# Second layer: the third head's q and k projections listed ahead of the attention's first scores, around the transposes of the RWKV output

## The chip, the cores and the metric

One core of a Trainium2 chip runs the whole kernel; seven cores stand idle. The metric is the device time in microseconds (us) of one execution. The kernel before took 1156.28 us as the median of three runs, which were 1147.5, 1156.28 and 1362.1 us.

## What is computed

Two layers of a hybrid backbone run over 512 latent tokens and 256 context tokens of width 1024. Each layer normalises, modulates and projects the tokens once, then feeds three mixers: an RWKV-7 scan in both directions, a short convolution, and differential attention with four heads. Cut to what this case touches:

```python
h = rms_norm(x, pre_g) * (1.0 + scale[:, None, :]) + shift[:, None, :]
p_l = split_projection(h @ w_in)                  # latent; p_c the same for the context
y_rwkv_l, _ = rwkv_mixer(p_l[0:8], p_c[0:8], ...)  # scan, readout, times silu(z)
# differential attention, head by head: two score maps per head
s = einsum('bqhjd,bkhjd->bhjqk', q, k) * scale     # q and k with axial rotary positions
p = softmax(s, axis=-1)
attn = p[:, :, 0] - lam * p[:, :, 1]
o = einsum('bhqk,bkhe->bqhe', attn, v)             # then rms_norm, times silu(z)
y_l = concatenate([y_rwkv_l, y_conv_l, y_attn_l], axis=-1) @ w_out
```

In the second layer only the latent tokens are wanted at the end, so queries are 512 rows; keys are 512 latent and 256 context rows.

## The kernel before

All products run on TensorE in fp32r pairs: an operand is split into a high part and a low remainder, and one product takes three matmuls (high by high, low by high, high by low). `split` (L242 to L262) loads a weight piece of 128x512 on the queue of SyncE (L251, `wraw`), casts its high part on ScalarE (L258, `whi`) and subtracts on GpSimd (L261, `wlo`). Two `wraw` buffers and three `whi`/`wlo` pairs serve all pieces. One projection of 128 output channels (`proj_ch`) needs two pieces: 24 matmuls of 512 latent columns (`pcl`) and, for keys, 24 more of 256 context columns (`pcc`).

Projections are generators that are put on a list, `fq`. `fill(us)` draws so many nominal microseconds of matmuls from the front of that list, wherever the code wants TensorE to have something to do while another engine works. The scheduler then orders the instructions of each engine by program order as priority and by what its own model holds ready; inside the attention the matmuls are pinned to program order (`lin["on"]`).

For each head, `qk` (L1084 to L1102) projects q and then k, evicts them (ScalarE, L1090, `qkr`), copies rotated halves by four DMAs (L1095, `qks`), multiplies by the sine table on GpSimd (L1096) and by the cosine table on VectorE, adds, casts the high part on ScalarE (L1099), subtracts the low part on VectorE, and writes both parts to DRAM (L1101 and L1102, `qd`). `head_in` (L1135 to L1158) loads a head's parts back from there as `QS`, `KH`, `KL`.

The end of a layer goes so: `rwkv_scan`, then `rwkv_out`, which normalises the scan's output `Y` on VectorE, then calls `fill(F["o"])`, and transposes `Y` on TensorE (`yT`, 32 matmuls). Then come the first head's loads, `fill(1e9)` (everything that is left on the list), and `attention`. That one works on units of 128 query rows, x counting from -3: scores of unit x+3 into three PSUM banks (`sc`), row maxima on VectorE (`mx`), exponentials on ScalarE (`e`), the combination of both maps on VectorE and GpSimd, transposes (`aTp`) and the product with v (`av`). Up to x = -1, `scores` has only one buffer of three banks (`pr0`), so each unit's scores wait for the exponentials of the unit before. The second such buffer (`pr1`) takes the banks of the projections, once `fill(1e9)` at x = 0 has emptied the list. After `attention` stand the splits of the RWKV and convolution outputs (`y_split`: casts and subtractions into `lat` on VectorE and GpSimd), which the scheduler draws forward.

`attn_proj` returns three lists: q, k, v of heads one and two; the attention's gate (`z_gate`, four projections); and `[qk(2), qk(3)]`, the third and fourth head's q and k. Before the change the last list goes on `fq` just before `attention`. There, `fill(FA[0])` draws 16 us of it ahead of the first scores, and `fill(FA[1])` draws 6 us behind the scores of each of the first three units.

Of the kernel before, what the change touches and what calls it, by code (L numbers as in the profile page):

```python
# [51 lines left out]
ATB = 2  # L52
ORD = [(0,), (4, 5), (1,), (2,), (3,)]
F = dict(p=1.0, s=0.5, i=0.45, i2=0.45, m0=4, m3=3, m1=3, m2=4, a=0.2, b=0.6, c=0.4, n=0.6, o=8, o2=2)
FL = [dict(F), dict(F, p=1.2, c=0.19, n=0.38, m0=3.5, a=0.32, o=11.9)]
H0 = 99
KS = 3
MP = 'fc'
# [6 lines left out]
FA = (16,6)  # L65
# [41 lines left out]
def build(tc, A):  # L107
# [217 lines left out]
    def filler():  # L325
        while modq:
            try:
                next(modq[0])
                return
            except StopIteration:  # L330
                modq.pop(0)
# [63 lines left out]
    def chs(l, idxs):  # L395
        wseq.extend((l, 2 * i + j) for i in idxs for j in range(2))

    def toks(l, idx):
        wseq.extend((l, 2 * idx + j) for j in range(4))
# [56 lines left out]
    fq = []  # L456

    def fill(us):
        while us > 0 and fq:
            try:  # L460
                us -= next(fq[0])
            except StopIteration:
                fq.pop(0)
# [696 lines left out]
    def attention(l, lat, cx, pool, az_done, hd0):  # L1160
        last = l == L - 1
        li = 0.8 - 0.6 * math.exp(-0.3 * l)
        n = NL if last else NT
# [156 lines left out]
                heads[u["h"] + 1] = head_in(l, u["h"] + 1, pool)  # L1320

        lin["on"] = AL
        fill(FA[0])
        fins = []

        def at(i):
            return us[i] if 0 <= i < len(us) else None

        for x in range(-3, len(us)):
            u, p, c, e, w = at(x), at(x - 1), at(x + 1), at(x + 2), at(x + 3)  # L1330
# [122 lines left out]
    for l in range(L):  # L1453
        F.update(FL[l])
        last = l == L - 1
        n = NL if last else NT
# [20 lines left out]
        with tc.tile_pool(name=f"yy{l}", bufs=1, reuse_waits="tile") as yy:  # L1477
            with tc.tile_pool(name=f"rw{l}", bufs=1, reuse_waits="tile") as rw:
                if RO:
                    for tag, nw, nb in (("rT", 2 * NT, 1), ("pt", 512, PTB), ("km", 512, 3), ("bk", 1024, 2), ("iv", 512, 2),  # L1480
                                        ("Wv", 512, 1), ("od", 256, 2), ("invt", 112, 1), ("ms", 256, 1), ("zu", 256, ZUB), ("gs", 128, 2),
                                        ("pz", 128, 2), ("rt", 512, 2)):
                        rw.tile([P, nw], F32, tag=tag, bufs=nb, name="rsv")
                modq[:] = [mod_half(a, t, hf, rp[0], "R", pt="c") for a, t in ME[l] for hf in range(2)]
                st = rwkv_in(l, lat, cx, rw, yy, pre)
                while modq and not must:
                    filler()
                toks(l, I_V)
                chs(l, (I_ZR, I_ZR + 1))
                chs(l, range(I_CONV, I_CONV + 8))  # L1490
                ap1, ap2, az = attn_proj(l, lat, cx)
                fq[:] = must + [rwkv_v(l, lat, cx), z_gate(l, 2, zrd[l], 0.5, lat, cx), conv(l, lat, cx)] + ap1
                rwkv_scan(l, st, rw, lat, cx)
                fill(FO)
                modq[:] = [mod_half(a, t, hf, rw, "pt", pt="c") for a, t in ML[l] for hf in range(2)]
                fq.extend(ap2)
                yr = yy.tile([P, 2, NT], F32, tag="yr", name="yr")
                rwkv_out(l, st, yr, rw)
                if EH == 2:
                    hd0 = head_in(l, 0)  # L1500
                fill(1e9)
                if EH == 3:
                    hd0 = head_in(l, 0)
                while modq:
                    filler()
# [199 lines left out]
```

## Time and profile before

| | |
|---|---|
| median of three runs | 1156.28 us (1147.5 to 1362.1) |
| time of the profiled execution | 1150.33 us |
| its span, first to last instruction | 1148.3 us |
| TensorE busy | 1034.9 us, 90% |
| VectorE busy | 731.3 us, 64% |
| ScalarE busy | 523.7 us, 46% |
| GpSimd busy | 488.0 us, 42% |
| granted TensorE clock, mean | 0.973 |

Times in rows count from the span's start. The profiled execution's time is 2.0 us above its span. A row of the timeline names start, duration, engine, line, operation, output and inputs; brackets give the idle time before it and what ended it. A row that stands for several instructions gives their count. Line L134 is the helper through which matmuls are recorded, L118 that of VectorE, so tiles tell more than lines there.

### The profile page before, as it was taken

How to read it: one execution, taken by the hardware profiler on the slowest of the kernel's cores; microseconds unless marked ns; L12 is line 12 of the kernel's file. 1: busy time of each engine (PE TensorE's matmuls, PEld its weight loads, DVE VectorE, ACT ScalarE, POOL GpSimd, SP SyncE). 2: the span in 40 equal slices, each digit the busy share in tenths (PEclk: the TensorE clock that was granted, in tenths of full speed). 3: DMA queues.
4: the chain of work that ended last, by engine and by line, in shares of the span. 5: the costliest groups of instructions: out<-in, count | busy, mean ns of one | idle time of the engine just before them, and what ended most of it. 6: DMA issues, size and time to landing. Idle time of an engine off the chain costs nothing.

```text
span 1148.3 us, 25449 instructions
## 1 busy us (share of the span) xinstructions
PE 1034.9 (90%) x9850; PEld 847.2 (74%) x9850; DVE 731.3 (64%) x1712; ACT 523.7 (46%) x1330; POOL 488.0 (42%) x508
## 2 busy tenths in 40 slices
PE   4899989999798999989899899998987999888897
PEld 1577968777687877878787786866766897777775
DVE  3530658687666253499847857676986824579944
ACT  4332462452362232378723564654343533338731
POOL 1311534434625422464522346254474454456632
PEclk9899999999899999999999999999998999999999
DMA  9573322212423365754052452232232345555143
GB/s 350 182 245 121 89 73 57 61 31 87 141 73 112 121 189 175 223 165 108 15 188 74 147 167 88 71 100 78 72 97 85 92 132 150 165 158 170 47 156 110
DMA packets 92088, 142.55 MB, mean 124 GB/s; under 512 B 28192, under 2 KB 36416, under 8 KB 91968
## 3 DMA queue, kind: packets, MB, share of 16 engines
q1 hardware_dynamic: 88512, 136.14, 38.4%
q10 hardware_dynamic: 3456, 4.80, 1.3%
q8 instruction: 77, 1.26, 0.5%
q14 instruction: 43, 0.35, 0.1%
HBM read 110.99 MB, written 25.71 MB: 119 GB/s over the span
## 4 chain that ended last, share of the span: by engine, by line
PE 36%; DVE 24%; ACT 6%; issue 6%; POOL 4%; DMA 3%; SPq 1%; DVEq 0%; ACTq 0%; POOLq 0%
PE pcl L134 10%; PE op L134 6%; PE ptl L134 4%; DVE mx L118 4%; PE pcc L134 2%; PE ptc L134 2%; PE ch L132 2%; DVE e L118 2%; DVE bk L118 2%; DVE rs_t L118 1%; DMA mraw<-in_mod_w_dram 1%; DVE qkr L118 1%; POOL wlo L261 1%; PE av L134 1%; PE yps L132 1%
## 5 line engine op out<-in xcount | busy, mean ns | idle before, releaser
L261 POOL TENSOR_TENSOR wlo<-wraw,whi 128x512 fp32r<-128x512 f32 x134 | 181.9, 1360 | 312.2 <-ACT whi L258 279.4
L134 PE MATMUL pcl<-lat,whi 128*128 128x512 f32 (+1 forms) x928 | 295.3, 395 | 1.0 <-POOL lat L344 0.8
L134 PEld LDWEIGHTS pcl<-lat,whi 128*128 128x128 f32 x928 | 170.2, 190 | 40.2 <-issue 6.4
L134 PE MATMUL pcl<-lat,wlo 128*128 128x512 f32 (+1 forms) x464 | 185.1, 399 | 5.1 <-POOL wlo L261 3.7
L258 ACT CAST whi<-wraw 128x512 fp32r<-128x512 f32 x144 | 88.4, 618 | 159.8 <-DMA wraw<-in_w_in_dram 38.5
L134 PE MATMUL pcc<-ctx,whi 128*128 128x256 f32 x576 | 112.8, 292 | 2.0 <-DVE ctx L118 1.7
L134 PEld LDWEIGHTS pcl<-lat,wlo 128*128 128x128 f32 x464 | 88.0, 190 | 28.2 <-POOL wlo L261 5.6
L134 PEld LDWEIGHTS pcc<-ctx,whi 128*128 128x128 f32 x576 | 95.2, 197 | 9.0 <-issue 3.2
L134 PE MATMUL pcc<-ctx,wlo 128*128 128x256 f32 x288 | 84.4, 293 | 2.0 <-DVE wlo L118 2.0
L134 PE MATMUL ptl<-whi,lat 128*128 128x256 f32 x384 | 82.0, 299 | 1.1 <-ACT qkr L1090 1.1
L1222 ACT ACTIVATE e<-sc,mx 128x768 f32<-128x768 f32 (+1 forms) x80 | 66.5, 834 | 19.5 <-DVE mx L118 14.0
L118 DVE TENSOR_REDUCE mx<-sc 128x1 f32<-128x768 f32 (+1 forms) x72 | 63.7, 918 | 14.0 <-PE sc L134 14.0
L134 PE MATMUL av<-vA,aT 128*128 128x128 f32 x416 | 59.6, 287 | 14.0 <-ACT aT L1257 13.8
L134 PEld LDWEIGHTS av<-vA,aT 128*128 128x128 f32 x416 | 54.2, 195 | 20.9 <-ACT aT L1257 17.9
L134 PEld LDWEIGHTS ptl<-whi,lat 128*128 128x128 f32 x384 | 65.4, 201 | 3.4 <-ACT qkr L1090 1.4
L118 DVE TENSOR_TENSOR R<-s,cs 128x384 f32<-128x384 f32 (+1 forms) x96 | 47.0, 529 | 20.9 <-PE s L132 20.2
L134 PEld LDWEIGHTS pcc<-ctx,wlo 128*128 128x128 f32 x288 | 56.7, 197 | 4.6 <-DVE wlo L118 2.2
L134 PE MATMUL ptl<-wlo,lat 128*128 128x256 f32 x192 | 57.6, 300 | 0.0
L920 POOL TENSOR_TENSOR pz<-zu,pc 64x128 f32<-64x128 f32 x88 | 37.4, 425 | 45.9 <-DVE zu L118 41.1
L134 PE MATMUL sc<-KH,QS 128*128 128x256 f32 (+1 forms) x144 | 51.4, 371 | 4.7 <-ACT e L1222 2.9
L134 PE MATMUL sc<-KL,QS 128*128 128x256 f32 (+1 forms) x144 | 45.0, 334 | 0.0
L1233 POOL TENSOR_TENSOR e<-e,cf 128x256 f32<-128x256 f32 x32 | 26.3, 823 | 42.0 <-DVE cf L118 13.9
(449 smaller groups left out, 2450.6 us busy)
## 6 DMA issues: line engine op xcount, KB each, us to landing
wraw<-in_w_in_dram SPq DMA_DIRECT2D x144, 256.0 KB, 2.7
mraw<-in_mod_w_dram SPq DMA_DIRECT2D x96, 256.0 KB, 4.6
KH<-qd SPq DMA_DIRECT2D x32, 192.0 KB, 4.1
oraw<-in_w_out_dram SPq DMA_DIRECT2D x20, 256.0 KB, 3.7
qd<-qks SPq DMA_DIRECT2D x12, 384.0 KB, 2.4
qd<-qkr SPq DMA_DIRECT2D x12, 384.0 KB, 2.5
qks<-qkr SPq DMA_DIRECT2D x64, 64.0 KB, 2.1
zu<-vd SPq DMA_DIRECT2D x96, 32.0 KB, 2.2
```

The lines of the kernel that those rows point to most:

```text
L118: i = f(*a, **k)
L132: tc.keep_in_program_order(nc.tensor.matmul(*a, **k))
L134: i = nc.tensor.matmul(*a, **k)
L258: S.copy(hi, raw)
L261: eng.tensor_tensor(out=lo, in0=raw, in1=hi.bitcast(F32), op=ALU.subtract)
L920: G.tensor_tensor(out=pz[d][hr], in0=zu[d][hr, :, h, :], in1=prepd[d][1][hr, :, cc[d][1]].unsqueeze(2).to_broadcast([64, 2, HD]), op=ALU.mult)
L1222: ac(S.activation(ej[:, c], pb[:, c], AF.Exp, bias=mx[:, i:i + 1], accum_out=den[:, u["h"] * 6 + tt, j:j + 1]))
L1233: G.tensor_tensor(out=e1, in0=e1, in1=cf[:, 0:1].to_broadcast([P, NC]), op=ALU.mult)
```

## The change

In the second layer `fill(FA[0])` ahead of the first scores is left out, the third head's q and k generator (`az.pop(0)` is `qk(2)`) goes on the list together with the gate, before `rwkv_out`, and the share that `rwkv_out` draws ahead of its transposes grows from 11.9 to 17.5 nominal us. `fill(FO)`, `fill(1e9)` and the fourth head's `qk(3)` stay where they were.

```diff
-FL = [dict(F), dict(F, p=1.2, c=0.19, n=0.38, m0=3.5, a=0.32, o=11.9)]
+FL = [dict(F), dict(F, p=1.2, c=0.19, n=0.38, m0=3.5, a=0.32, o=17.5)]
...
         lin["on"] = AL
-        fill(FA[0])
+        if not last:
+            fill(FA[0])
...
                 fq.extend(ap2)
+                if last:
+                    fq.append(az.pop(0))
                 yr = yy.tile([P, 2, NT], F32, tag="yr", name="yr")
                 rwkv_out(l, st, yr, rw)
```

No instruction is added or removed. In the built programs every row of TensorE up to the end of the third head's context columns is at the same place: 53 `pcl` matmuls, the 32 transposes `yT`, 46 `pcl` (the rest of the third head's q, and its k), 24 `pcc`. The larger share does not move the transposes. The programs part behind that.

On TensorE, at the first unit's scores, the program before has the first 16 matmuls of the fourth head's q (tile `pcl_12275`) ahead of them:

```order
L134 MATMUL pcl_12275<-lat0_112,wlo_12214 128x512
L134 MATMUL pcl_12275<-lat0_112,whi_12245 128x512
L134 MATMUL pcl_12275<-lat1_113,whi_12245 128x512
L134 MATMUL pcl_12275<-lat0_112,wlo_12246 128x512
L134 MATMUL pcl_12275<-lat0_112,whi_12245 128x512
L134 MATMUL sc_12298<-KH0_12042,QS0_12040 128x512
L134 MATMUL sc_12298<-KL0_12044,QS0_12040 128x512
```

The changed program has the third head's last context columns there:

```order
L134 MATMUL pcc_12201<-ctx0_114,wlo_12179 128x256
L134 MATMUL pcc_12201<-ctx0_114,whi_12178 128x256
L134 MATMUL pcc_12201<-ctx1_115,whi_12178 128x256
L134 MATMUL pcc_12201<-ctx0_114,wlo_12179 128x256
L134 MATMUL sc_12273<-KH0_12087,QS0_12085 128x512
L134 MATMUL sc_12273<-KL0_12089,QS0_12085 128x512
L134 MATMUL sc_12273<-KH0_12087,QS0_12085 128x256
```

The 16 matmuls now stand behind these scores. Between the first and the second unit's scores are 29 `pcl` in both programs. Between the second and the third unit's are 3 `pcl` and 24 `pcc` before, and 19 `pcl` and 19 `pcc` now; 5 `pcc` come behind the third unit's scores. Of the 19 `pcl`, the first 7 use the first weight piece of the fourth head's k, and the last 12 its second piece, which is the last weight piece of this stage (`wraw_12346` before, `wraw_12382` now).

On SyncE's queue that last piece is, before, the last row with `wraw`. It stands ahead of the third head's q going to DRAM (`qd<-qks` and `qd<-qkr` of 512 columns) and well ahead of its k (768 columns):

```order
L1156 DMA KH_12381<-qd_96 64x768
L251 DMA wraw<-in_w_in_dram 128x512
L1101 DMA qd_96<-qks 128x512
L1102 DMA qd_96<-qkr 128x512
L1156 DMA KH_12381<-qd_96 64x768
L1095 DMA qks<-qkr 32x512 x4
L1157 DMA KL_12383<-qd_96 64x768
L1154 DMA QS_12380<-qd_96 64x512 x2
L1156 DMA KH_12382<-qd_96 64x768 x2
L1101 DMA qd_96<-qks 128x768
L1102 DMA qd_96<-qkr 128x768
```

In the changed program the same stretch of the queue reads:

```order
L1156 DMA KH_12359<-qd_96 64x768 x2
L1101 DMA qd_96<-qks 128x512
L1102 DMA qd_96<-qkr 128x512
L1157 DMA KL_12361<-qd_96 64x768
L1095 DMA qks<-qkr 32x512 x4
L1154 DMA QS_12358<-qd_96 64x512 x2
L1156 DMA KH_12360<-qd_96 64x768 x2
L1157 DMA KL_12362<-qd_96 64x768
L1101 DMA qd_96<-qks 128x768
L1102 DMA qd_96<-qkr 128x768
L251 DMA wraw<-in_w_in_dram 128x512
```

The load of the last piece moved from ahead of the third head's q to behind its k.

On GpSimd, before, the low parts of the last three pieces (`wlo`) stand together, ahead of the sine product of the third head's k:

```order
L1096 TENSOR_TENSOR qks<-qks,sinT 128x512
L261 TENSOR_TENSOR wlo<-wraw,whi 128x512 x3
L1096 TENSOR_TENSOR qks<-qks,sinT 128x512
L344 TENSOR_TENSOR lat_113<-yr,lat_112 128x512
L344 TENSOR_TENSOR lat_113<-yc,lat_112 128x512
L1152 MEMSET KL_12591 64x768
L1233 TENSOR_TENSOR e_12364<-e_12364,cf 128x256
L1234 TENSOR_TENSOR e_12362<-e_12362,e_12364 128x256
```

In the changed program the same stretch of GpSimd is:

```order
L261 TENSOR_TENSOR wlo<-wraw,whi 128x512 x2
L1096 TENSOR_TENSOR qks<-qks,sinT 128x512
L1233 TENSOR_TENSOR e_12342<-e_12342,cf 128x256
L1234 TENSOR_TENSOR e_12340<-e_12340,e_12342 128x256
L344 TENSOR_TENSOR lat_113<-yr,lat_112 128x512
L344 TENSOR_TENSOR lat_113<-yc,lat_112 128x512
L1152 MEMSET KL_12591 64x768
L261 TENSOR_TENSOR wlo<-wraw,whi 128x512
```

The low part of the last piece moved behind the first unit's combination, two splits and a fill.

On ScalarE the cast of the last piece (`whi`) stood ahead of the first unit's exponentials and now stands behind the second unit's. On VectorE, from the first unit's maxima on, the order is now: `lat` cast and subtraction, cosine product of the third head's k, first maximum of the second unit, sum of the k rotation, second maximum, low part of that k, first unit's coefficient `cf`, a `lat` cast, the first unit's combination, two `lat` casts and a subtraction, the whole rotation of the fourth head's q, third unit's maxima. Before, all of the k rotation and the `lat` work stood between the first and the second unit's maxima, and the rotation of the fourth head's q stood behind the third unit's maxima.

## Rows read from the trace of the kernel before

**Rows 1.** The page of the profile: shares of the chain that ended last, by engine.

```profile
PE 36%; DVE 24%; ACT 6%; issue 6%; POOL 4%; DMA 3%; SPq 1%; DVEq 0%; ACTq 0%; POOLq 0%
```

**Rows 2.** Busy time by stage: stretch and its length, then busy us (and count) of PE, PE weight load, VectorE, ScalarE and GpSimd, granted TensorE clock, DMA share, GB/s.

```profile
987.00:989.70 2.70, 2.65 (x64) 2.58 (x64) 1.80 (x3) 0.72 (x1) 0.34 (x1) 0.73 0.26 88
989.70:991.60 1.90, 1.90 (x7) 1.50 (x6) 0.69 (x1) 0.00 (x0) 0.00 (x0) 0.50 1.00 220
1020.90:1023.80 2.90, 0.02 (x2) 0.02 (x1) 1.90 (x4) 1.95 (x5) 1.47 (x2) 1.00 0.81 265
1025.50:1091.00 65.50, 54.31 (x378) 48.07 (x377) 63.36 (x135) 50.16 (x138) 40.13 (x43) 0.97 0.37 111
```

**Rows 3.** The chain that ended last, in order of time: start, length, engine, tile and line, count.

```profile
1001.37 2.87 PE pcc L134 x24
1004.24 3.65 PE pcl L134 x16
1007.90 1.42 PE sc L134 x8
...
1020.03 1.73 DVE mx L118 x2
```

**Rows 4.** Timeline of TensorE, from the transposes `yT` to the third unit's scores.

```profile
987.05 2.73 PE L134 MATMUL yT<-ident,Y 64*64 64x64 f32 x64 [3.52 <-DVE Y L118]
...
990.31 1.05 PE L134 MATMUL pcl<-lat,whi 128*128 128x512 f32 x2
991.16 0.62 PE L134 MATMUL pcl<-lat,wlo 128*128 128x512 f32 x1
...
1004.08 0.63 PE L134 MATMUL pcl<-lat,whi 128*128 128x512 f32 x2
...
1007.73 0.40 PE L134 MATMUL sc<-KH,QS 128*128 128x512 f32 x1
...
1009.15 0.39 PE L134 MATMUL pcl<-lat,whi 128*128 128x512 f32 x1
...
1015.77 0.40 PE L134 MATMUL sc<-KH,QS 128*128 128x512 f32 x1
...
1017.18 0.63 PE L134 MATMUL pcl<-lat,whi 128*128 128x512 f32 x2
...
1020.62 0.28 PE L134 MATMUL pcc<-ctx,wlo 128*128 128x256 f32 x1
1023.78 0.50 PE L134 MATMUL sc<-KH,QS 128*128 128x512 f32 x1 [2.88 <-ACT e L1222]
```

**Rows 5.** Timeline of VectorE, from the second unit's stage on.

```profile
1009.35 1.82 DVE L118 TENSOR_REDUCE mx<-sc 128x1 f32<-128x768 f32 x2 [4.04 <-PE sc L134]
1011.89 0.43 DVE L118 CAST lat<-yr 128x512 fp32r<-128x512 f32 x1 [0.71 <-PE pcl L134]
...
1012.96 1.78 DVE L118 TENSOR_TENSOR qkr<-qkr,cosT 128x512 f32<-128x512 f32 x1
...
1015.00 0.68 DVE L118 TENSOR_TENSOR qkr<-qkr,qks 128x512 f32<-128x512 f32 x1
...
1027.30 1.77 DVE L118 TENSOR_TENSOR qkr<-qkr,cosT 128x512 f32<-128x512 f32 x1
...
1029.90 1.10 DVE L118 TENSOR_TENSOR qkr<-qkr,qks 128x512 f32<-128x512 f32 x1
...
1031.79 0.67 DVE L118 TENSOR_TENSOR qkr<-qkr,qks 128x512 fp32r<-128x512 f32 x1
...
1045.19 0.95 DVE L118 TENSOR_TENSOR qkr<-qkr,qks 128x768 fp32r<-128x768 f32 x1
```

**Rows 6.** Timeline of ScalarE: the cast of the last weight piece, and that of the third head's k.

```profile
1007.83 0.62 ACT L258 CAST whi<-wraw 128x512 fp32r<-128x512 f32 x1 [2.72 <-DMA wraw<-in_w_in_dram]
...
1015.75 0.83 ACT L1099 CAST qks<-qkr 128x768 fp32r<-128x768 f32 x1 [2.19 <-issue]
```

**Rows 7.** Timeline of GpSimd, from the low part of the last weight piece on.

```profile
1008.58 1.30 POOL L261 TENSOR_TENSOR wlo<-wraw,whi 128x512 fp32r<-128x512 f32 x1 [2.12 <-ACT whi L258]
1012.57 1.62 POOL L1096 TENSOR_TENSOR qks<-qks,sinT 128x512 f32<-128x512 f32 x1 [2.69 <-DMA qks<-qkr]
1015.15 1.69 POOL L344 TENSOR_TENSOR lat<-yr,lat 128x512 fp32r<-128x512 f32 x1 [0.96 <-DVE lat L118]
1017.53 1.68 POOL L344 TENSOR_TENSOR lat<-yc,lat 128x512 fp32r<-128x512 f32 x1 [0.69 <-DVE lat L118]
1019.27 0.74 POOL L1152 MEMSET KL<- 64x768 f32 x1
1022.25 1.09 POOL L1233 TENSOR_TENSOR e<-e,cf 128x256 f32<-128x256 f32 x1 [2.24 <-DVE cf L118]
1023.42 0.73 POOL L1234 TENSOR_TENSOR e<-e,e 128x256 f32<-128x256 f32 x1
```

**Rows 8.** Timeline of SyncE's queue: the load of the last weight piece, the third head's k rotation, and its k going to DRAM.

```profile
1004.78 0.33 SPq L251 DMA_DIRECT2D wraw<-in_w_in_dram  x1
...
1008.49 2.44 SPq L1095 DMA_DIRECT2D qks<-qkr  x4
...
1016.61 0.33 SPq L1101 DMA_DIRECT2D qd<-qks  x1
1020.06 0.33 SPq L1102 DMA_DIRECT2D qd<-qkr  x1
```

## The prediction

> **What bounds the kernel now.** I read the page first. Its chain of work [rows 1] goes 36% through TensorE and 24% through VectorE, so the limit changes by stage, and the stage of the change must be read alone. The table by stage [rows 2] gives it: from 1025.5 to 1091 us, the attention of the second layer, VectorE is busy 63.36 of 65.50 us (97%) and TensorE 54.31 (83%). There VectorE's queue sets the pace. Ahead of it TensorE does: the chain in order of time [rows 3] runs through its `pcc`, `pcl` and first `sc` rows without a break, then crosses to VectorE, where the second unit's maxima start only at 1020.03. The timeline of TensorE [rows 4] shows two waits: 3.52 us for `Y` ahead of the transposes, and 2.88 us ahead of the third unit's scores at 1023.78, which wait for the second unit's exponentials, since both use the same three banks.
>
> **What does not change.** TensorE's order is the same up to and behind the transposes, so the 3.52 us for `Y` stay: the larger share in `rwkv_out` costs and brings nothing. In both programs the third head's q and k already stand ahead of the first scores. No instruction is added, and behind the attention all is the same work on TensorE. What moves are 16 matmuls of the fourth head's q, from ahead of the first scores to behind them, and, with other priorities, the load, cast and low part of the fourth head's last weight piece.
>
> **The first scores come earlier.** The 16 matmuls take 3.65 us on the chain [rows 3], 0.228 us each. Without them the first scores start at 1004.08, where the first of the 16 stands [rows 4], instead of 1007.73. VectorE had been idle 4.04 us ahead of the first maxima [rows 5], so it can take them that much earlier. The scores take 1.42 us and end at 1005.50. Then 29 `pcl` follow as before, 1009.15 to 1015.77 or 6.62 us [rows 4]: second scores 1012.12 to 1013.53. Then 7 `pcl` of the first k piece, 7 x 0.228 = 1.6 us: at 1015.13 TensorE needs the last piece.
>
> **The last weight piece comes later.** Before, SyncE issued it at 1004.78 [rows 8], its cast began at 1007.83 [rows 6], 3.05 us later, and its low part ended at 1009.9 [rows 7], long before use. Now it stands on SyncE behind the write of the third head's k, a queue in order, so the k rotation must end first. I walk that with the durations of rows. VectorE's first `lat` cast waits for TensorE to be done with the first block in the fourth head's k, the 27th `pcl`: before 1009.15 + 11 x 0.228, now 1005.50 + 27 x 0.228, both 1011.66. So it stays at 1011.89, and the cosine product at 1012.96 to 1014.74 [rows 5]; its 1.78 us come from the sine product on GpSimd, 1012.57 to 1014.19 [rows 7], which waits for the rotation's DMAs of 1008.49 [rows 8], which the change leaves alone. Then VectorE's new order: a maximum (1.82 / 2 = 0.91), the sum (0.68), a maximum (0.91), to 1017.24; ScalarE's cast of 0.83 [rows 6] runs beside the second; the low part takes 0.95, as in the undisturbed row of 1045.19 [rows 5]: 1018.2. SyncE writes both parts and issues the load at about 1018.6. The cast starts 3.05 us later, 1021.65, and ends 0.62 later at 1022.3. TensorE waits from 1015.13 to 1022.3, 7.2 us.
>
> Queued behind that cast on ScalarE are the cast of the fourth head's q, two evictions, and the first `aT` copy; behind the load on SyncE, the rotation of the fourth head's q. They start later too, and none is needed before the third unit's scores, except the eviction of the last context columns (its `pr1` banks), some 0.4 us with its wait.
>
> Two matmuls use the high part; the third needs the low part. On GpSimd this stands behind the first unit's combination, which needs the coefficient that VectorE computes only after the k rotation, about 1018.5. By rows: 1.09 + 0.73 + 1.69 + 1.68 + 0.74 + 1.30 = 7.2 us [rows 7], so 1025.7. That is a second wait of about 2.5 us. Then 10 `pcl` and 19 `pcc` (2.87 / 24 = 0.12 each [rows 3]): 2.28 + 2.28 us. The third unit's scores start at 1030.3, against 1023.78: a lag of **6.5 us** at full clock. The five `pcc` behind them lie beside VectorE's maxima.
>
> **Clock.** After the wait of 3.52 us the granted clock was 0.73 and then 0.50, which is 1.2 GHz, up to 991.6 [rows 2]; `pcl` matmuls there came every 0.425 us [rows 4]. After 2.88 us it stayed 1.00 [rows 2]. The wait here is 7.2 us, so it lies beyond the one that lowered it. Ten `pcl` at 0.425 instead of 0.228 cost **2.0 us** more; nothing if the clock is back, and 19 x 0.12 = 2.3 us on top if the `pcc` are slow too. I take 2.0, by the nearer row.
>
> **What is given back.** While TensorE waits, VectorE does what stood behind the third scores: the rotation of the fourth head's q, 1.77 + 1.10 + 0.67 = 3.5 us as it stood beside GpSimd, 3 x 0.68 = 2.0 us by the undisturbed row [rows 5]. Since VectorE's queue sets the pace afterwards, what leaves it is regained. The most is 3.5 us plus its idle 65.50 - 63.36 = 2.1 us [rows 2], 5.6 in all; the least is nothing, if the units are bound by their chain of scores, maxima, exponentials. I take **2.0**.
>
> **Sum.** 6.5 + 2.0 - 2.0 = +6.5 us on the profiled execution's 1150.33: 1156.8, or **1157 us**. With the bounds: 6.5 + 0 - 5.6 = +0.9, and 6.5 + 4.3 - 0 = +10.8, so 1151.2 to 1161.1. The profiled execution lies 2.8 us above the lowest run and 5.9 under the median of the runs shown, a spread as large as the change; the range has to hold that too.
>
> **Rivals.**
> - *The last piece is not late, and the first scores' lead arrives: faster.* It decides at one point: the cast of the piece would have to begin by 1014.5, so its load be issued by 1011.5, and the third head's k be written by then. For it: the lead of 3.65 us is real, and VectorE is idle ahead of the first maxima. Against it: the cosine product of that k did not start before 1012.96, held by a DMA [rows 7] that does not move. It gives 1150.33 - 3.65 = 1146.7. Chance 0.08.
> - *Nearly all is given back.* VectorE fills TensorE's waits, then runs without its 2.1 us of idle time, and the clock is not lowered: +0.9, or 1151.2. For it: the 97%. Against it: in those waits VectorE itself waits for that same late piece, since the second rotation and the third maxima hang on it. Chance 0.20.
> - *The clock stays low through the second wait,* so the context columns are slow too: 6.5 + 4.3 - 2.0 = +8.8, or 1159.1. For it: 7.2 and 2.5 us of wait with two matmuls between. Against it: a wait of 2.88 us lowered nothing. Chance 0.16. The Trainium skill, "TensorE: Matmul & The Clock Gate", section "HAM oscillation — how this bites in real kernels", says that a wait for DMA between bursts of matmuls lets the clock fall back each time, and each burst then starts cold. By that rule this rival is the case and the sum is its 1159.1; the row of 2.88 us speaks against the rule for the shorter wait, those of 3.52 us for it.
>
> The Trainium skill, "SBUF — State Buffer", section "SBUF: two separate sides", gives the reason for rows like the 1.78 us product: VectorE and GpSimd hold one pair of ports in turn, for a whole instruction. By it GpSimd's 7.2 us in front of the low part would grow by VectorE's casts in between, which no row here prices for the new order.
>
> **Chances.** My forecast has 0.54, the rivals 0.08, 0.20 and 0.16; 0.02 is for what I don't see. The range 1150 to 1166 leaves out the fast rival and a part of the second, and reaches above 1161.1 by most of the 5.9 us between profiled execution and median. The likeliest case alone is 1154 to 1161. All cases lie within 2% of the time before (23 us), about what a measurement of this kernel can tell from no change: faster 0.01, within 0.96, slower 0.03.
>
> **What would show it.** In the profile of the changed kernel: the first scores about 3.6 us earlier behind the transposes; the last `wraw` issued behind the k write, near 14 us after the first scores; a wait of TensorE of about 7 us ended by ScalarE's `whi`, a second of 2 to 3 us ended by GpSimd's `wlo`, `pcl` rows near 0.43 us apart behind them; the third scores some 8 us later than now; less of that at the end of the attention. I am wrong if the last piece is there in time, if the k rotation runs earlier than walked, or if VectorE's queue is so loose behind the waits that the lag is gone by the last unit.

## The result, and the profile after

The changed kernel took 1162.17 us as the median of 6 runs (1156.18 to 1171.42), beside 1153.77 us for the kernel before on the same chip; the ratio is 1.013, with a 95% interval of 1.0092 to 1.0169. (The run of 1362.1 us of the kernel before is left out of the ratio; without it the median before is 1152.01 us, and the two medians alone give 1.009.) So the change costs about 1%, within the 2% that the prediction called no change and more than its +6.5 us. The median lies inside the predicted range, but above the 1161.1 us of the sum's own upper bound. The profiled execution took 1156.18 us, its span is 1154.4 us. That this is so near the 1156.8 us of the sum is luck, as the next paragraph shows.

The profiled executions can be compared more closely than the medians. Both programs have the same work on TensorE up to the transposes, and there both are at the same granted clock: 0.64 over the 4.70 us from the transposes' start. That start is at 987.05 in the profile before and at 982.79 after; the 4.26 us between them lie ahead of the change. From it to the end of the span it is 1148.3 - 987.05 = 161.25 us before and 1154.4 - 982.79 = 171.61 after: **+10.36 us**. TensorE's timeline after, which answers to [rows 4]:

```profile
982.79 2.92 PE L134 MATMUL yT<-ident,Y 64*64 64x64 f32 x64 [3.52 <-DVE Y L118]
...
999.78 0.40 PE L134 MATMUL sc<-KH,QS 128*128 128x512 f32 x1
...
1007.81 0.40 PE L134 MATMUL sc<-KH,QS 128*128 128x512 f32 x1
...
1017.26 1.22 PE L134 MATMUL pcl<-lat,whi 128*128 128x512 f32 x2 [6.26 <-ACT whi L258]
...
1020.55 0.79 PE L134 MATMUL pcl<-lat,wlo 128*128 128x512 f32 x1 [2.07 <-POOL wlo L261]
...
1027.14 0.40 PE L134 MATMUL sc<-KH,QS 128*128 128x512 f32 x1
...
1038.20 1.54 PE L134 MATMUL av<-vA,aT 128*128 128x128 f32 x6 [2.36 <-ACT aT L1257]
```

The first scores come 16.99 us behind the transposes' start instead of 20.68, 3.69 us earlier. Two waits for the last weight piece follow, 6.26 us for its high part and 2.07 us for its low part. The third scores stand 44.35 us behind the transposes instead of 36.73: they lag by 7.62 us. A third wait, at 1038.20, has no counterpart of its length behind the third scores before.

Why the piece is late shows on SyncE, ScalarE and GpSimd (timelines after; [rows 8], [rows 6] and [rows 7] before):

```profile
1012.90 0.33 SPq L1102 DMA_DIRECT2D qd<-qkr  x1
1013.27 0.46 SPq L251 DMA_DIRECT2D wraw<-in_w_in_dram  x1
```

```profile
1016.59 0.62 ACT L258 CAST whi<-wraw 128x512 fp32r<-128x512 f32 x1 [2.78 <-DMA wraw<-in_w_in_dram]
...
1036.06 0.90 ACT L1222 ACTIVATE e<-sc,mx 128x768 f32<-128x768 f32 x1 [2.01 <-DVE mx L118]
...
1036.95 0.82 ACT L1099 CAST qks<-qkr 128x768 fp32r<-128x768 f32 x1
1037.67 0.48 ACT L1257 COPY aT<-aTp 128x384 f32<-128x384 f32 x1
```

```profile
1013.15 0.66 POOL L1233 TENSOR_TENSOR e<-e,cf 128x256 f32<-128x256 f32 x1 [5.82 <-DVE cf L118]
1013.89 1.05 POOL L1234 TENSOR_TENSOR e<-e,e 128x256 f32<-128x256 f32 x1
1014.90 1.44 POOL L344 TENSOR_TENSOR lat<-yr,lat 128x512 fp32r<-128x512 f32 x1
1016.70 1.66 POOL L344 TENSOR_TENSOR lat<-yc,lat 128x512 fp32r<-128x512 f32 x1 [0.36 <-DVE lat L118]
1018.42 0.73 POOL L1152 MEMSET KL<- 64x768 f32 x1
1019.24 1.26 POOL L261 TENSOR_TENSOR wlo<-wraw,whi 128x512 fp32r<-128x512 f32 x1
```

The load stands right behind the write of the third head's k and goes out at 1013.27, 13.49 us behind the first scores; before, it went out 2.95 us ahead of them. The cast waits for the data, and the low part is the sixth instruction in GpSimd's row of work.

VectorE's timeline after ([rows 5] before), from the third head's k rotation to the fourth unit:

```profile
1008.62 0.68 DVE L118 TENSOR_TENSOR qkr<-qkr,cosT 128x512 f32<-128x512 f32 x1
...
1018.15 0.76 DVE L118 TENSOR_TENSOR qkr<-qkr,cosT 128x512 f32<-128x512 f32 x1 [0.93 <-DMA qks<-qkr]
1021.76 0.69 DVE L118 TENSOR_TENSOR qkr<-qkr,qks 128x512 f32<-128x512 f32 x1 [2.85 <-POOL qks L1096]
1023.18 0.69 DVE L118 TENSOR_TENSOR qkr<-qkr,qks 128x512 fp32r<-128x512 f32 x1 [0.73 <-ACT qks L1099]
1028.74 1.82 DVE L118 TENSOR_REDUCE mx<-sc 128x1 f32<-128x768 f32 x2 [4.87 <-PE sc L134]
...
1032.69 0.94 DVE L118 TENSOR_REDUCE mx<-sc 128x1 f32<-128x768 f32 x1
1033.55 1.60 DVE L118 TENSOR_TENSOR qkr<-qkr,cosT 128x512 f32<-128x512 f32 x1
1035.08 0.95 DVE L118 TENSOR_REDUCE mx<-sc 128x1 f32<-128x768 f32 x1
```

In TensorE's first wait, 1011.00 to 1017.26, VectorE is busy nearly all the time (6.22 of 6.26 us, first line of the next table), with the end of the third head's k rotation, the first unit's combination and the `lat` work. Between that wait and the third unit's maxima at 1028.74 it has only the fourth head's q rotation (1018.15 to 1023.87, 2.1 us of work) and is idle for the rest: 0.93 + 2.85 + 0.73 + 4.87 = 9.4 us. Then the fourth head's k rotation comes between the two maxima of the fourth unit. Before, its cosine product stood 15.7 us behind the third unit's maxima (VectorE's timeline before):

```profile
1041.19 1.21 DVE L118 TENSOR_TENSOR qkr<-qkr,cosT 128x512 f32<-128x512 f32 x1
```

The table by stage after ([rows 2] before; columns as there):

```profile
1011.00:1017.26 6.26, 0.00 (x1) 0.00 (x0) 6.22 (x9) 3.32 (x6) 3.67 (x4) 0.78 0.59 199
1028.70:1097.00 68.30, 56.45 (x383) 50.20 (x382) 64.89 (x132) 49.63 (x137) 37.18 (x41) 0.95 0.28 80
1017.19:1020.79 3.60, 1.46 (x3) 0.74 (x4) 0.80 (x2) 0.02 (x1) 3.46 (x4) 0.50 0.56 156
1020.79:1023.79 3.00, 3.00 (x8) 2.32 (x9) 1.30 (x2) 0.62 (x1) 0.94 (x1) 0.50 0.57 165
1038.79:1042.79 4.00, 4.00 (x21) 3.71 (x21) 2.98 (x6) 2.58 (x10) 1.77 (x3) 0.63 0.91 304
```

In the attention VectorE is busy 64.89 of 68.30 us (95%), nearly as before, so this share alone tells little of what was lost. The granted clock is 0.50, 1.2 GHz, behind the waits for the piece, and 0.63 again behind the wait of 2.36 us. The chain in order of time after ([rows 3] before) prices the first of these:

```profile
1020.55 4.47 PE pcl L134 x10
1025.02 2.27 PE pcc L134 x19
```

Ten `pcl` take 4.47 us, 2.2 us more than 10 x 0.228, and the context columns are at full speed again.

The lag doesn't stay at 7.62 us. The sixteenth and last unit's scores start at 1079.81 before and at 1085.53 after (TensorE's timelines):

```profile
1079.81 0.48 PE L134 MATMUL sc<-KH,QS 128*128 128x512 f32 x1
```

```profile
1085.53 0.48 PE L134 MATMUL sc<-KH,QS 128*128 128x512 f32 x1
```

That is 72.08 us behind the first scores before and 85.75 us after. With the lead of 3.69 us that is a lag of 9.98 us: 2.36 us more were lost among the units in between, where the prediction had 2.0 us given back.

### The profile page after: what moved, and what is told of

Its sections match the earlier page's. It is cut to its first block, busy times and chain, and to the rows that moved or that the text cites. A ratio compares the mean times of both kernels' runs of the same rounds, so it can differ in the third digit from the quotient of the medians.

```text
span 1154.4 us, 25444 instructions
## 1 busy us (share of the span) xinstructions
PE 1037.6 (90%) x9850; PEld 848.1 (73%) x9850; DVE 732.5 (63%) x1712; ACT 524.1 (45%) x1330; POOL 484.9 (42%) x508
## 4 chain that ended last, share of the span: by engine, by line
PE 36%; DVE 24%; ACT 6%; issue 5%; POOL 3%; DMA 3%; SPq 1%; ACTq 0%; DVEq 0%; POOLq 0%
PE pcl L134 11%; PE op L134 6%; PE ptl L134 4%; DVE mx L118 3%; PE pcc L134 2%; PE ptc L134 2%; DVE bk L118 2%; PE ch L132 2%; DVE e L118 2%; DVE rs_t L118 2%; PE av L134 1%; DMA mraw<-in_mod_w_dram 1%; POOL wlo L261 1%; PE yps L132 1%; DVE Acc L118 1%
## 5 line engine op out<-in xcount | busy, mean ns | idle before, releaser
L134 PE MATMUL pcl<-lat,whi 128*128 128x512 f32 (+1 forms) x928 | 298.9, 399 | 8.0 <-ACT whi L258 6.3
L134 PE MATMUL pcc<-ctx,whi 128*128 128x256 f32 x576 | 110.2, 288 | 2.3 <-DVE ctx L118 1.7
```

The lines of the kernel that those rows point to most:

```text
L134: i = nc.tensor.matmul(*a, **k)
```

## The experiments

The question was whether the late piece makes the loss, or the moved matmuls with VectorE's new order, and why the lag grew. Each kernel is compared with the kernel before, run on the same chip. Beside its ratio the table has two lags from the traces, in us: of the third unit's scores and of the last unit's scores, each counted from the first scores of its own trace against that of before (16.05 and 72.08 us), less the lead of 3.70 us where TensorE's order is that of the change. Counted so, the granted clock ahead of the first scores, which differs by trace, drops out. An edit sets less than it seems to: the scheduler orders all engines anew. In the traces low_on_dve keeps the change's order on every engine but for the one moved instruction; warm_both and k_rot_behind move a cast on ScalarE and two transfers on SyncE besides what is said of them; early_piece, late_alone and warm_whi have another order on VectorE, ScalarE, GpSimd and SyncE at many places.

| kernel | third | last | ratio | 95% interval |
|---|---|---|---|---|
| the change | 7.6 | 10.0 | 1.0130 | 1.0092 to 1.0169 |
| change_again | 7.7 | 9.8 | 1.0133 | 1.0096 to 1.0169 |
| o_undone | 7.6 | 9.7 | 1.0062 | 1.0032 to 1.0093 |
| early_piece | -3.7 | -0.9 | 1.0005 | 0.9973 to 1.0037 |
| late_alone | 8.9 | 9.7 | 1.0061 | 1.0024 to 1.0097 |
| low_on_dve | 6.3 | 8.5 | 1.0065 | 1.0042 to 1.0088 |
| warm_wait | 9.0 | 12.6 | 1.0114 | 1.0062 to 1.0166 |
| warm_whi | 7.3 | 6.9 | 1.0045 | 1.0019 to 1.0071 |
| warm_both | 5.8 | 6.1 | 1.0056 | 1.0028 to 1.0085 |
| k_rot_behind | 7.7 | 7.8 | 1.0069 | 1.0036 to 1.0101 |
| warm_and_rot | 5.8 | 6.1 | 1.0054 | 1.0033 to 1.0075 |
| early_light | -3.7 | 1.5 | 1.0025 | 0.9996 to 1.0054 |
| early_wo | -3.7 | 0.3 | 1.0036 | 1.0007 to 1.0066 |

### The late piece: early_piece and late_alone

The last piece listed early again, in the change:

```diff
                 t, sw = fst("qkr"), fst("qks")
+                if last and h == 3 and i == 1:
+                    prefetch()
```

> The change, with the load, cast and low part of the fourth head's last weight piece listed again early, where the fourth head's k projection begins; TensorE's order is that of the change. Theory (the late piece is the loss): TensorE waits for no whi or wlo between the second and the third scores, its clock stays at 1.00 there, the first scores keep their lead of 3.7 us, and the time is 0.997 to 1.000 of the kernel before (-3.65 us if the lead arrives, 0 if VectorE's queue eats it). Rival (the moved matmuls and VectorE's new order, with the fourth head's rotation among units 4 and 5, are the loss): the wait is gone and the time stays at 1.008 to 1.013.

```profile
1005.84 0.33 SPq L251 DMA_DIRECT2D wraw<-in_w_in_dram  x1
```

```profile
1005.14 0.40 PE L134 MATMUL sc<-KH,QS 128*128 128x512 f32 x1
...
1021.20 0.40 PE L134 MATMUL sc<-KH,QS 128*128 128x512 f32 x1
```

SyncE's and TensorE's timelines: the load goes out 0.70 us behind the first scores, and the third scores follow the first by 16.06 us, as before (16.05), without a wait that the timeline shows, where before 2.88 us of it were a wait. The time is that of the kernel before, 1.0005. So with the piece in time TensorE's new order costs nothing that can be measured. Whether VectorE's new order would, is not shown by this kernel, which has an order of its own there. The lead of 3.7 us at the third unit is 0.9 us at the last, and the last unit's scores are followed by 1.7 us more than before up to the end. That VectorE doesn't use the lead shows on its timeline:

```profile
1012.90 0.43 DVE L118 CAST lat<-yr 128x512 fp32r<-128x512 f32 x1 [4.34 <-PE pcl L134]
```

The first `lat` cast waits 4.34 us for the matmuls that now stand behind the first scores; the idle time of 4.04 us ahead of the first maxima [rows 5] has moved there.

The other way round, the kernel before with that load alone put behind the k write on SyncE:

```diff
+        if lin.get("behind") and tag == "w" and not wseq:
+            tc.add_manual_dep(ld.ins, lin["behind"], ...)
...
+                if last and h == 2 and i == 1:
+                    lin["behind"] = wr.ins.name
```

> The kernel before, with nothing changed but SyncE's order: the load of the last piece stands behind the write of the third head's k, as in the change. There TensorE needs the piece ahead of the second scores, at about 1013.7; the k rotation lets the load go at about 1017.5, the cast ends at 1021: a wait of some 7.4 us, and 2 to 3 us of half clock. Theory (the late piece is the loss): 1.006 to 1.010 of the kernel before. Rival (VectorE's queue takes in what the wait costs, and the loss of the change is due to the moved matmuls): 1.000 to 1.003.

```profile
1017.31 1.22 PE L134 MATMUL pcl<-lat,whi 128*128 128x512 f32 x2 [8.47 <-ACT whi L262]
```

TensorE's timeline has a wait of 8.47 us, one us longer than expected. The last unit lags by 9.7 us, as in the change, and the ratio is 1.0061. So a late piece makes a loss like that in the change's trace, with no matmul moved. It is not SyncE's order alone, though: the trace shows that the scheduler answered with another order on VectorE, ScalarE and GpSimd too (the first three `lat` casts stand ahead of the k rotation's sum, the `w_out` pieces come earlier).

### The second wait: low_on_dve

The low part of that piece on VectorE:

```diff
         eng = G if wcount[0] % 2 == (tag != "m") or pool_only else V
+        if lin.pop("lowv", False):
+            eng = V
...
+            lin["lowv"] = l == L - 1 and lin["on"] and not wseq
```

> The change, with the low part of that last piece on VectorE instead of GpSimd, where it stood behind the first unit's combination and two low parts of lat; nothing else moves. VectorE is free when the cast ends, so the low part ends about 2.4 us earlier: TensorE's second wait, 2.07 us, is gone. Theory (nothing of the waits is given back, since VectorE has nothing left to do in them): third scores 2 us earlier and the end too, some 0.2% under the change. Rival (VectorE's queue gives waits back): the end moves by under 1 us.

```profile
1016.28 1.22 PE L134 MATMUL pcl<-lat,whi 128*128 128x512 f32 x2 [6.06 <-ACT whi L258]
...
1018.19 0.80 PE L134 MATMUL pcl<-lat,wlo 128*128 128x512 f32 x1 [0.69 <-DVE wlo L118]
```

The second wait is 0.69 us instead of 2.07, not gone, since the subtraction took 1.76 us on VectorE beside GpSimd's work. The third scores come 1.3 us earlier than in the change and the last 1.5: what is taken from TensorE's waits here (1.38 us of the second, 0.20 of the first) is worth its full length. At the last unit nothing of it had been given back.

### The clock: warm_wait, warm_whi and warm_both

Matmuls in the wait, whose result nobody reads:

```diff
+NWARM = 24
...
+                    if lin["on"] and l == L - 1 and k == 4 and cx is not None and not wseq:
+                        dm = ps("a", "dum")
+                        for z in range(NWARM):
+                            T.matmul(dm, ws[0][0][:, 0:P], lat[0][:, z % 4, 0:512], start=True, stop=True)
```

> The change, with 24 matmuls of 128x512 whose result nobody reads put into TensorE's wait for the last piece (24 x 0.228 = 5.5 us into a wait of 6.26 us). Theory (the half clock behind the wait is part of the loss): the pcl behind the wait come every 0.228 us instead of 0.425, the third scores come 2 to 2.5 us earlier than in the change, and the time is 2 to 2.5 us less than that of the change: 1.010 to 1.011 of the kernel before. If that slow stretch lies beside work of VectorE that has to be done anyway, the scores come earlier and the time stays at 1.013. If the clock doesn't hang on what TensorE does in the wait, both stay.

This edit did not do what was meant: the 24 matmuls stood a second time ahead of the context columns, and read `lat`, so that VectorE's cast into `lat` waited 2.67 us for them. Its last unit lags by 12.6 us, and it says nothing of the clock. Mended, with the weight piece as both operands and once only:

> The change, with 24 matmuls of 128x512 in TensorE's wait for the last piece, as in warm_wait, but once only (warm_wait had them a second time ahead of the context columns, where nothing waits) and with operands that nobody writes (there they read lat, whose casts on VectorE had to wait for them). Theory (the half clock behind the wait is part of the loss): the granted clock is 1.00 when the piece comes, the ten pcl behind it take 2.0 us less, the third scores start about 42.3 us behind the transposes' start instead of 44.35, and the attention ends 2 to 3.5 us earlier than in the change. Rival (the slow stretch is covered by VectorE's rotation): the third scores come earlier, the end of the attention does not.

```profile
1018.15 5.61 PE L134 MATMUL dum<-whi 128*128 128x512 f32 x24
1024.59 0.73 PE L134 MATMUL pcl<-lat,whi 128*128 128x512 f32 x2 [0.83 <-ACT whi L258]
1027.92 0.80 PE L134 MATMUL pcl<-lat,wlo 128*128 128x512 f32 x1 [2.59 <-POOL wlo L261]
```

```profile
1028.12:1031.12 3.00, 3.00 (x8) 2.32 (x9) 0.69 (x1) 0.00 (x0) 0.97 (x1) 0.50 0.55 170
```

The timeline and the table by stage: the clock held to the second wait, then 2.59 us of waiting brought 0.50 after all, so the third scores gained only 0.3 us where 2 were expected. The last unit gained 3.1 us nevertheless. VectorE's order is not that of the change in this kernel: the fourth unit's maxima stand together, ahead of the k rotation. That led to k_rot_behind. To ask for the clock alone, both waits were filled (24 and 12 matmuls), which leaves VectorE's order as in the change:

```diff
+                    if dm is not None and w is lo:
+                        for z in range(12):
+                            T.matmul(dm, ws[0][0][:, 0:P], ws[0][0], start=True, stop=True)
+                        dm = None
```

> The change, with matmuls that nobody reads in both of TensorE's waits for the last piece: 24 ahead of the first matmul that needs its high part and 12 (2.7 us) ahead of the first that needs its low part. VectorE's, ScalarE's and GpSimd's order are those of the change but for one cast. warm_whi, which filled the first wait only, kept 1.00 up to the second wait and fell to 0.50 behind it, so its third scores came only 0.3 us earlier. Theory (the half clock behind the waits costs what the ten pcl at 0.425 say): granted clock 1.00 from the second scores to the third, third scores 2 us earlier than in the change, and as much at the end of the attention, so about 8 us above the kernel before, 1.007. If VectorE covers it: third scores earlier, the end as in the change, 10 us, 1.009.

```profile
1018.08:1021.08 3.00, 3.00 (x17) 2.58 (x18) 1.22 (x2) 1.18 (x2) 1.02 (x1) 1.00 0.91 244
```

The clock is 1.00 in the stretch that had 0.50. The third scores come 1.8 us earlier than in the change; the last 3.9 us. The half clock behind the waits is worth what the ten `pcl` say, and the growth of the lag is nearly gone too (5.8 us at the third unit, 6.1 at the last): the wait for `aT` is 0.90 us here instead of 2.36. The clock need not be the reason of that. VectorE's order is the change's, and the fourth head's cosine product stands between the same two maxima, but it takes 0.83 us here instead of 1.60:

```profile
1028.58 0.83 DVE L118 TENSOR_TENSOR qkr<-qkr,cosT 128x512 f32<-128x512 f32 x1
```

```profile
1032.63 0.94 PE L134 MATMUL av<-vA,aT 128*128 128x128 f32 x6 [0.90 <-ACT aT L1266]
```

### The growth of the lag: k_rot_behind and warm_and_rot

The fourth head's k rotation kept back until both maxima of the unit are listed:

```diff
+                def rot(t=t, sw=sw, i=i):
...
+                if last and h == 3 and i == 1:
+                    lin["rot"] = rot
...
                 maxi(w, 1)
+                if lin.get("rot") and x >= 0:
+                    lin.pop("rot")()
```

> The change, with the cosine product and the sum of the fourth head's k moved behind the pair of maxima of the fourth unit, between which the product stood; nothing else moves on TensorE, ScalarE and GpSimd. Between the third unit's scores and the last, the change loses another 2.4 us (lag 7.6 to 10.0), and the rows show a wait of TensorE of 2.36 us for aT at 1038 and half clock behind it, to 1042. Theory A (the product between the maxima holds up the exponentials, and the wait and the clock follow from it): that wait shrinks to under 1.5 us and the end of the attention comes 1.5 to 3 us earlier than in the change. Theory B (the growth comes from the half clock behind the late piece, or from VectorE's queue in general): the end stays within 1 us of the change.

```profile
1045.26 1.81 DVE L118 TENSOR_REDUCE mx<-sc 128x1 f32<-128x768 f32 x2
1047.00 0.73 DVE L118 TENSOR_TENSOR qkr<-qkr,cosT 128x512 f32<-128x512 f32 x1
```

```profile
1053.86 0.94 PE L134 MATMUL av<-vA,aT 128*128 128x128 f32 x6 [1.35 <-ACT aT L1262]
```

The result is theory A's. With the maxima together (VectorE's timeline) no wait of TensorE up to the last unit's scores is longer than 1.35 us, its clock is 1.00 from the third maxima on, and the lag at the last unit is what the third scores left: 7.7, then 7.8 us, 2.1 us less than in the change. In the change the product of 1.60 us stands between the maxima, ScalarE's exponential waits 2.01 us for the second of them, the k cast and then the copy of `aT` stand behind it, TensorE waits 2.36 us for that copy, and its clock falls to 0.63. In k_rot_behind ScalarE's cast of that k moved behind the copy as well, against the expectation that nothing else moves, so the product's share and the cast's are not told apart.

> warm_both and k_rot_behind in one: both waits for the last piece filled with matmuls that nobody reads, and the fourth head's cosine product and sum behind the pair of maxima. By warm_both the third scores lag the kernel before by 5.8 us at full clock. Theory (of that lag nothing is given back and, with the product out of the way, nothing is added): the end of the attention lags by 5.3 to 6.3 us, the time is 1.004 to 1.006 of the kernel before. Rival (VectorE gives back some 2 us of it, as the prediction had it): a lag of 3 to 4.5 us at the end. If warm_both's clock alone did all that k_rot_behind did, the end is warm_both's, 6.5.

The last unit lags by 6.1 us, as in warm_both. The end of the span, counted from the transposes, lags by 7.7 us, above what any theory had and 1.3 us behind warm_both. That is lost behind the last unit's scores, and the traces show where: in both TensorE waits about 2.25 us for `aT` there, and the clock behind that wait is lower and longer so in warm_and_rot. In k_rot_behind, behind the same wait, it doesn't fall. The rows of six us from the end of that wait, in warm_both, warm_and_rot and k_rot_behind:

```profile
1086.40:1092.40 6.00, 5.70 (x32) 4.88 (x33) 3.60 (x9) 3.28 (x12) 3.47 (x4) 0.72 0.00 0
1091.48:1097.48 6.00, 6.00 (x26) 5.48 (x27) 3.59 (x9) 2.46 (x8) 3.46 (x4) 0.50 0.00 0
1103.42:1109.42 6.00, 5.14 (x38) 4.36 (x39) 3.60 (x9) 3.62 (x12) 3.48 (x4) 1.00 0.01 3
```

So the two don't add: either edit keeps the lag from growing up to the last unit. In sum nothing of the 5.8 us is given back there. On the way some is: in warm_and_rot the lag is 4.2 us at the ninth unit's scores (the kernel before takes 5.25 us from the eighth unit's to these, with its fourth head's k rotation there, against 3.79) and 6.3 us again at the eleventh's. What takes it back was not tested.

### The rest: o_undone, change_again, early_light, early_wo

The number `o` back at 11.9, and the change once more:

> The change with the other number, o, back at 11.9. The instructions and their order are those of the change on every engine but for two neighbouring transfers on SyncE, so every theory of the moved matmuls expects 1.013 again, within its interval of 1.009 to 1.017; a time near 1.000 would say that the number, or the state of the chip, made the difference.

> The change itself, timed once more beside the others, since it came out at 1.013 (1.009 to 1.017) and the all but equal program of o_undone at 1.006 (1.003 to 1.009). By the traces of both, 10.0 to 10.4 us are lost behind the transposes, so 1.009 is expected; 1.006 or less would say that part of the lag in the traces is not in the median run, 1.012 or more that something ahead of the transposes is slower too.

Both traces repeat the lags of the change within 0.4 us. The ratios do not agree: 1.0133 again for the change, 1.0062 for the all but equal program. By the traces' +10.0 to +10.4 us it should be 1.009 for both. The plain medians scatter around that: 10.2 us above the kernel before for the change (without the run of 1362.1 us), 13.8 for change_again, 7.6 for o_undone. What lies ahead of the transposes varies by more than that: they start between 980.08 and 995.30 us in the profiled executions of all these kernels, with the same work on TensorE ahead of them. Why the two ratios of the change come out some 5 us above its traces, and that of o_undone some 3 us below, stays open; the change has six runs each time, o_undone twelve.

If VectorE sets the pace, work taken from it should give early_piece its lead:

```diff
-(V if h in QV else G).tensor_tensor(...)
+(V if h in QV and not (last and h == 3) else G).tensor_tensor(...)
...
-                              out_pool=pool)
+                              out_pool=pool, pool_only=last and k < WN)
```

> early_piece, with VectorE lightened: the cosine products and low parts of the fourth head's q and k and the low parts of three w_out pieces go to GpSimd, in the second layer alone. By rows of the kernel before that takes 2 x 0.68 + 0.67 + 0.95 + 3 x 0.67 = 5.0 us from VectorE. Theory (early_piece's lead of 3.7 us was lost because VectorE's queue sets the pace of the attention): the attention ends 3 to 5 us earlier than in early_piece, 0.996 to 0.998 of the kernel before. Rival (the units are bound by their chain of scores, maxima, exponentials and copies, or GpSimd, 44 of 75 us busy, becomes the one that is waited for): 1.000 or above.

> early_piece, with the low parts of three w_out pieces on GpSimd instead of VectorE, in the second layer alone: the part of early_light that left the fourth head's rotation alone (there the rotation on GpSimd ended in a wait of 2.9 us ahead of the tenth unit). It takes 3 x 0.67 = 2.0 us from VectorE. Theory (VectorE's queue sets the pace): the attention ends about 2 us earlier than in early_piece, 0.998 to 0.999 of the kernel before. Rival (the units are bound by their chain): as early_piece, 1.000 to 1.001.

(early_wo has the second edit only.) What the theory of VectorE's pace expected did not come: with an estimated 5 us, and 2 us, less to do there, the last unit came 2.4 and 1.1 us later than in early_piece. It is no clean refutation, since the work went to GpSimd and new waits arose. In early_light TensorE waits 2.90 us ahead of the tenth unit; in early_wo its clock is 0.76 for 7 us behind a wait of 2.02 us, where early_piece has 1.00 behind 2.40 us. In both a wait of 4.2 us for `aT` behind the last unit's scores, 1.97 us in early_piece, costs more, and at the end of the span, counted from the first scores, they lag by 5.1 and 3.4 us (early_piece by 0.8). Which of these waits and clocks eats the lead was not taken apart. No kernel here beats the one before.

## Why the prediction was wrong

- **What does not change** held: the wait of 3.52 us for `Y` is still there, and the larger share ahead of the transposes brings nothing: o_undone, without it, repeats the change's trace.
- **The first scores come earlier**: -3.65 us forecast, -3.69 measured.
- **The last weight piece comes later**: the place on SyncE, both waits and what each engine has queued were as walked. Waits of 7.2 and 2.5 us were forecast, 6.26 and 2.07 measured. (By its own numbers the walk gives 2.9 for the second, 1025.7 less 1022.3 and two matmuls; the sum did not use it.) The cosine product took 0.68 us instead of the 1.78 I carried over. I had left the rotation's DMAs in their place, but they went out 19.17 us behind the transposes' start instead of 21.44, and GpSimd's sine product was done (1006.04 to 1007.33) before the cosine product began. That product did not begin earlier for it, 25.83 us behind the transposes against 25.91: what held it was the `lat` work ahead of it, and not the DMA that I named against the fast rival. GpSimd's work from the first unit's combination to the end of the low part took 7.35 us (1013.15 to 1020.50), 7.2 in the sum. TensorE's two waits in the change, early_piece and late_alone show that the late piece is the cause of the lag at the third scores.
- **Clock**: +2.0 forecast; the ten `pcl` cost 2.2, and warm_both's third scores gained 1.8. With it the third scores lag by 7.62 us; 6.5 + 2.0 = 8.5 were forecast. The rival of a clock that stays low through the context columns did not come: 19 `pcc` in 2.27 us. The Trainium skill, "TensorE: Matmul & The Clock Gate", section "HAM oscillation — how this bites in real kernels", tells of a kernel in which the wait for a DMA is long enough that each burst of matmuls behind it starts cold. The wait of 6.26 us in the change agrees (0.50 behind it). The 2.88 us before do not speak against the page, as the prediction has it, since the page does not say it of every wait.
- **What is given back**: this is the step that failed. I took 2.0 us as regained; 2.36 us more were lost up to the last unit. With the third scores 0.9 us better than forecast and 0.4 us lost behind the last unit's scores, +6.5 became +10.4. Of the bounds that I set, "the least is nothing" was near the truth and still too good. I read a VectorE that is busy 97% of the attention as one that would profit from every early start. In TensorE's first wait it had no time to spare (6.22 of 6.26 us busy). Behind it, it did bring the fourth head's q rotation forward, 2.1 us of work, but was idle for 9.4 us around its links, because that rotation's DMAs stand behind the load on SyncE, its sine product behind the low part on GpSimd, and the third maxima behind the same late piece. I had named this against a rival and not against my own 2.0. And what left the queue behind the third scores was replaced: the k rotation of the same head moved up into the fourth unit, 4.8 us behind the third maxima instead of 15.7, where another wait and another half clock followed; with it out of the way (k_rot_behind) the 2.36 us are not lost. low_on_dve and warm_and_rot show that at the last unit TensorE's waits are worth their full length. That holds for the trace; the rest of the ratio of 1.013, some 5 us, stays open.
- **Rivals**: the fast one has its condition in early_piece, the piece in time, and would still not have come: its 3.65 us are 0.9 at the last unit and nothing in the time. The one where nearly all is given back is refuted by low_on_dve, k_rot_behind and warm_and_rot, the last with the clock at 1.00 from the wait to the last unit's scores.

## What to carry to other kernels

Moving matmuls cost nothing measurable here as long as the weights were in time (early_piece). What can move with them is the point at which a weight load is listed, and here that load landed on SyncE's queue behind a write that waited for a long chain. Before crediting a busy engine with using a wait, list what it could run in that wait that doesn't hang on the same late thing; if there is nothing, the wait counts in full. And ask where the work that is brought forward will stand next: here a rotation with its product of 1.6 us between two links of the chain that paces the loop cost about 2 us, by a wait and the clock behind it, and nearly nothing where the same product took 0.83 us (warm_both). A single trace of one kernel can carry a us or two of clock by chance, as the next section shows, so a lag is best read ahead of such a place and beside a second trace.

## What the hardware showed that I had not expected

The same wait of 3.52 us ahead of the transposes, with the same work on either side, was followed by a granted clock of 0.64 or less over 4.70 us in 11 of 14 traces and of 1.00 in 3; early_piece, one of the 3, has its first scores 1.54 us earlier behind the transposes than the change (15.45 and 16.99 us). Waits of 2.59 and 2.36 us were followed by 0.50 (warm_whi) and 0.63 (the change), one of 2.88 us before by 1.00 (table by stage before, behind the wait of [rows 4]):

```profile
1023.80:1027.00 3.20, 3.20 (x21) 2.88 (x22) 1.51 (x2) 1.17 (x3) 0.80 (x2) 1.00 0.40 106
```

The wait of about 2.25 us behind the last unit's scores, which ten of the traces have at the same place, was followed over six us by 0.72 in five (the change among them), by 0.50 in warm_wait and warm_and_rot, and by 1.00 in late_alone, warm_whi and k_rot_behind. So in these traces the length of one wait doesn't tell whether the clock will fall. Filling both waits for the piece with matmuls did keep it at 1.00 (warm_both).
